# Expert weights of a two-layer mixer block loaded as pairs of tiles with 8 KB rows

## The chip, the cores and the metric

The kernel runs on one core of a Trainium2 chip. The metric is the device time of one execution in microseconds (us); less is better. TensorE, VectorE, ScalarE, GpSimd and SyncE are called PE, DVE, ACT, POOL and SP as the profile does; PEld is the weight load of a matmul.

## What is computed

Two layers of a hybrid mixer over 256 latent and 256 context tokens of width 1024. The change concerns the channel mixer of the second layer, which sends each of the 256 latent tokens to 2 of 8 experts:

```python
def _swiglu(h, w_gate, w_up, w_down):
    return (jax.nn.silu(h @ w_gate) * (h @ w_up)) @ w_down

def _moe(h, router, w_gate, w_up, w_down):
    t = h.reshape(-1, shape[-1])
    logits = (t @ router).astype(jnp.float32)
    top_val, top_idx = lax.top_k(logits, TOP_K)          # TOP_K = 2
    top_w = jax.nn.softmax(top_val, axis=-1)
    gate = jnp.sum(jax.nn.one_hot(top_idx, N_EXPERTS) * top_w[..., None], axis=1)
    out = jnp.zeros_like(t)
    for e in range(N_EXPERTS):                           # 8 experts, hidden width 3584
        out = out + gate[:, e:e + 1] * _swiglu(t, w_gate[e], w_up[e], w_down[e])
```

All weights are float32. One expert's three matrices are 44 MB, the eight together 352 MB.

## The kernel before

**The first 930 us** are layer 0 (attention, a gated recurrence, a gated spatial unit, a dense SwiGLU) and the mixers of layer 1. Their weights come through `Stream` (line 73): a raw 512 KB tile is loaded and split by ACT and DVE into a high and a low part, which PE multiplies in three passes. A scheduler sets the order of every engine there.

**Memory.** `Mem` (line 39) holds lists of free 4 KB, 2 KB and 1 KB slots (bytes per partition); a slot that is given back goes to the end of its list, and the next taker gets the one at the front. There are 34 slots of 4 KB from the start (line 1843). When the mixers of layer 1 are done, the pool of the small slots is closed and 16 more slots of 4 KB take its place (lines 1952 to 1954).

**The expert layer** (`moe_layer`, line 1964) loads every expert's weights whole and gathers the tokens of an expert (up to 96) by a matmul with a one-hot matrix (`moe_gather`, line 1537). An expert is four units: units 0 to 2 take 1024 hidden columns each, unit 3 the last 512. `gate_up` (line 1585) does the two input products of a unit in two halves, `turned` (line 1613) transposes the result on PE, and `moe_down` (line 1631) multiplies it with the rows of the output matrix one unit later. So a unit of 1024 columns consumes 16 weight tiles in `gate_up` and 8 in `moe_down`, unit 3 takes 8 and 4: 84 tiles of 512 KB for an expert, 672 in all. The matmuls take the weights as the moving operand, 512 (unit 3: 256) columns for 32 tokens, four column groups of PE side by side (`four`, line 1571).

An expert with at most 64 tokens can leave out a third of this work. `arms` (line 1578) writes both versions into the program and branches between them:

```python
        with self.tc.If(self.third[e] > 0) as c:
            yield 1
        with c.Else():
            yield 0
```

In this input experts 0, 2, 4, 6 and 7 take the long arm and experts 1, 3 and 5 the short one. `moe_add` (line 1668) scatters an expert's result back to the tokens with two blocks of four matmuls (`t<-yhl,ohT`, line 1682); it is a generator that `paced` (line 1972) moves on by one step for each step of `gate_up` and `moe_down`, and it begins only when `Mem` has two free slots (`mem.room`, line 1671). In the expert layer PE's order is the order of the program.

**The ring.** `Ring` (line 161) loads the expert weights in the order of a list that `moe_plan` (line 1770) makes. `need(n)` hands out the next n tiles and first gives back the slots of the tiles handed out before:

```python
    def load(self):
        while self.n_dma < len(self.plan) and self.free:
            slot = self.free.popleft()
            r = slot.tile([P, 1024], F32, name=f"wr{self.n_dma}")
            self.tiles[self.n_dma] = r, slot
            self.nc.sync.dma_start(r, self.plan[self.n_dma])
            self.n_dma += 1
```

It gets its slots in three steps: the three raw slots of `Stream` when its list is through (`heir`, line 136), 25 at line 1955 and 2 at line 1961, which leaves 14 slots to the rest of the expert layer. So the ring has 30 tiles. All its loads are issued by SP. Each DMA takes one of 8 semaphores in turn, and SP waits for the DMA that held it before, so at most 8 loads are under way.

Of the kernel before, what the change touches and what calls it, by code (L numbers as in the profile page):

```python
# [9 lines left out]
F32 = mybir.dt.float32  # L10
# [25 lines left out]
TTS = (2, 3, 0, 1)  # L36


class Mem:


    def __init__(self):
        self.free = {4: deque(), 2: deque(), 1: deque()}
        self.used = {}

    def add(self, pool, kb, n, mark=""):
        self.free[kb].extend(pool.ring(1024 * kb, name=f"m{mark}{kb}_{i}") for i in range(n))

    def get(self, kb, shape, name, dt=F32):
        slot = self.free[kb].popleft()  # L50
        n = int(np.prod(shape[1:]))
        t = slot.tile([P, (512 if dt == BF16 else 256) * kb], dt, name=name)[:, :n]
        if len(shape) > 2:
            d = "abcd"[:len(shape) - 1]
            t = t.rearrange(f"p ({' '.join(d)}) -> p {' '.join(d)}", **{x: int(m) for x, m in zip(d, shape[1:])})
        self.used[id(t)] = kb, slot, t
        return t
# [15 lines left out]
class Stream:  # L73
# [3 lines left out]
    def __init__(self, nc, plan, mem, raw, hl):  # L77
        self.nc, self.plan, self.mem = nc, plan, mem
        self.n_dma = self.n_split = self.n_out = self.n_done = self.part = 0
        self.raw, self.hl = {}, {}  # L80
        self.raw_free, self.hl_free = deque(), deque()
        self.heir = None
        self.excess = 0
        self.grow(raw, hl)

    def grow(self, raw, hl):

        free = self.mem.free[4]
        self.raw_free.extend(free.popleft() for _ in range(raw))
        self.hl_free.extend((free.popleft(), free.popleft()) for _ in range(hl))  # L90

    def close(self):

# [21 lines left out]
    def step(self):  # L115
        i, nc = self.n_split, self.nc
        w = self.plan[i][1]
        r, slot = self.raw[i]
        if self.part == 0:
            s = self.hl_free.popleft()  # L120
            self.hl[i] = [x.tile([P, 1024], F32R, name=f"{t}{i}") for x, t in zip(s, ("hi", "lo"))] + [s]
        h, l, _ = self.hl[i]
        s = slice(0, min(w, 512)) if self.part == 0 else slice(512, w)
        if s.stop > s.start:
            nc.scalar.activation(h[:, s], r[:, s], AF.Copy)  # L125
            nc.vector.tensor_tensor(l[:, s], r[:, s], h[:, s].bitcast(F32), op=ALU.subtract)  # L126
        self.part += 1
        if self.part == 2:
            self.part = 0
            self.n_split += 1  # L130
            del self.raw[i]
            if self.n_dma < len(self.plan):
                self.raw_free.append(slot)
                self.load()
            else:
                self.heir.free.append(slot)
                self.heir.load()

    def tick(self, n=1):
        for _ in range(n):  # L140
# [20 lines left out]
class Ring:  # L161
# [4 lines left out]
        self.n_dma = self.n_out = 0  # L166
        self.free, self.tiles, self.held = deque(), {}, []

    def grow(self, n):
        for _ in range(n):  # L170
            self.free.append(self.mem.free[4].popleft())
        self.load()

    def load(self):
        while self.n_dma < len(self.plan) and self.free:
            slot = self.free.popleft()
            r = slot.tile([P, 1024], F32, name=f"wr{self.n_dma}")
            self.tiles[self.n_dma] = r, slot
            self.nc.sync.dma_start(r, self.plan[self.n_dma])
            self.n_dma += 1  # L180

    def need(self, n):
# [6 lines left out]
        return [r for r, _ in got]  # L189

    def close(self):
        self.mem.free[4].extend(self.held)
        self.mem.free[4].extend(self.free)
        self.held, self.free = [], deque()


class Gen:
# [1387 lines left out]
    def gate_up(self, e, x, u, h):  # L1585


        nc = self.nc
        n = 512 if u < 3 else 256
        G, U, X = (self.psum("u") for _ in range(3))  # L1590
        for half in range(2):
            w = [t.rearrange("p (k n) -> p k n", k=2) for t in self.ring.need(8 if u < 3 else 4)]
            for arm in self.arms(e):
                for q in range(2):
                    v = w[4 * q:4 * q + 4] if u < 3 else [t[:, :, s:s + 256] for t in w[2 * q:2 * q + 2]
                                                          for s in (0, 256)]
# [34 lines left out]
    def moe_down(self, e, hT, u, yb, yx):  # L1631

        m = 4 if u < 3 else 2
        w = [(t[:, :512], t[:, 512:]) for t in self.ring.need(2 * m)]
        for arm in self.arms(e):
            if u == 0 and not arm:
                self.four(yx, 512, ((self.zero, w[0][0]),) * 4, True, True)
# [64 lines left out]
    def moe_rest_expert(self, one, off, n):  # L1702
# [14 lines left out]
        py = [self.psum("mm") for _ in range(2)]  # L1717
        for c in range(7):
            pgu = []
            for nm in ("moe_g", "moe_u"):  # L1720
                ps = self.psum("u")
                for kq in range(4):
                    r = load(A[nm][one, c, kq].rearrange("o p k n -> p (o k n)"))
# [15 lines left out]
            self.done(pt)  # L1739
            mem.put(h)  # L1740
            for a in range(4):
                r = load(A["moe_d"][one, 4 * c + a].rearrange("o p n -> p (o n)"))
# [27 lines left out]
    def moe_plan(self):  # L1770

        A = self.A
        f = lambda ap: ap.rearrange("p a b -> p (a b)")
        plan = []
        for i in range(len(self.UNITS) + 1):
            if i < len(self.UNITS):
                e, u = self.UNITS[i]
                cs = (2 * u, 2 * u + 1) if u < 3 else (6,)
                plan += [f(A[nm][e, c, kq]) for kq in range(4) for nm in ("moe_g", "moe_u") for c in cs]
            if i:  # L1780
                e, u = self.UNITS[i - 1]
                m = 4 if u < 3 else 2
                plan += [A["moe_d"][e, 8 * u + m * b + j] for j in range(m) for b in range(2)]
# [52 lines left out]
    def build(self):  # L1836
        nc, tc, A = self.nc, self.tc, self.A
        with ExitStack() as ctx:
# [4 lines left out]
            mem.add(big, 4, N4)  # L1843
# [10 lines left out]
            self.ring = self.ws.heir = Ring(nc, self.moe_plan(), mem)  # L1854
# [60 lines left out]
            self.run(self.norm_mod(0, 24, (0,)))  # L1915
            self.run(self.ffn(), self.ada_columns())
            self.run(self.norm_mod(1, 0, (0,)))
            self.begin(1)
            proj = self.proj(1)
            self.tokens()  # L1920
# [30 lines left out]
            mem.free[1].clear()  # L1951
            c1.close()
            more = ctx.enter_context(tc.tile_pool(name="more", bufs=1, side="right"))
            mem.add(more, 4, N4B, "x")
            self.ring.grow(len(mem.free[4]) - 5)
            self.run(self.prep_tile(1, w1, rows["ga"]))
            mem.put(*self.mxt, rows["ga"])
            self.ws.close()
            self.moe_prep(rows["sh"], rows["sc"])
            self.gf = rows["gf"]  # L1960
            self.ring.grow(len(mem.free[4]) - 14)
            self.moe_layer()

    def moe_layer(self):
# [48 lines left out]
NF = 2  # L2013
PVC = ((0,), (0, 2))
N4, N2, N1 = 34, 12, 24
N4B = 16
GROW0 = 4
FSHR = 2
PSPARE = dict(mm=0, u=2)
# [49 lines left out]
def _layout(inp):  # L2069
# [23 lines left out]
    for n, s in (("moe_g", "moe_w_gate"), ("moe_u", "moe_w_up")):  # L2093
        d[n] = c(g[s][0].reshape(NE, 4, 2, P, 7, 512).transpose(0, 4, 1, 3, 2, 5))
    d["moe_d"] = c(g["moe_w_down"][0].reshape(NE, 28, P, D))
# [22 lines left out]
```

## Time and profile before

| | |
|---|---|
| median of 3 runs | 1843.02 us (1839.42, 1843.02, 6153.94) |
| the profiled execution | 1835.17 us |
| its span, first to last instruction | 1833.4 us |
| PE busy in the span | 1753.2 us, 96% |
| mean granted TensorE clock | 0.988 |
| read from HBM | 481 MB |

The profiled execution is 7.8 us shorter than the median. Busy time of PE is the union of its matmuls, whose ends are modelled; the queue q1 of the DMA table carries what SP issues, q8 the blocks of instructions that the engines fetch. A row of the timeline merges instructions of one line; the bracket behind it tells how long the engine was idle before it and what ended that.

### The profile page before, as it was taken

How to read it: one execution, taken by the hardware profiler on the slowest of the kernel's cores; microseconds unless marked ns; L12 is line 12 of the kernel's file. 1: busy time of each engine (PE TensorE's matmuls, PEld its weight loads, DVE VectorE, ACT ScalarE, POOL GpSimd, SP SyncE). 2: the span in 40 equal slices, each digit the busy share in tenths (PEclk: the TensorE clock that was granted, in tenths of full speed). 3: DMA queues.
4: the chain of work that ended last, by engine and by line, in shares of the span. 5: the costliest groups of instructions: out<-in, count | busy, mean ns of one | idle time of the engine just before them, and what ended most of it. 6: DMA issues, size and time to landing. Idle time of an engine off the chain costs nothing. (4 is left out here: it accounts for less than half of the span.)

```text
span 1833.4 us, 34728 instructions
## 1 busy us (share of the span) xinstructions
PE 1753.2 (96%) x14056; PEld 1084.3 (59%) x14057; DVE 778.5 (42%) x1924; ACT 537.7 (29%) x1203; POOL 33.3 (2%) x56
## 2 busy tenths in 40 slices
PE   6999999999999999999989998999989999999996
PEld 3999778988788898998843333333333333333332
DVE  4656877899755377868720011110212011120112
ACT  4654655723223256765410010100101011010100
POOL 1000000100000001000000000000000000000000
PEclk9999999999999999999989999999999999999998
DMA  9224342366763245230589999999999999999990
GB/s 347 73 83 147 114 150 80 117 241 226 240 221 134 97 143 182 89 127 13 196 316 379 402 406 407 406 407 400 402 400 406 404 402 402 400 407 404 403 392 31
DMA packets 137006, 485.64 MB, mean 265 GB/s; under 512 B 15888, under 2 KB 17040, under 8 KB 136784
## 3 DMA queue, kind: packets, MB, share of 16 engines
q1 hardware_dynamic: 136080, 480.08, 69.1%
q8 instruction: 168, 2.75, 0.6%
q0 software_dynamic: 704, 2.36, 0.4%
q14 instruction: 54, 0.44, 0.1%
HBM read 481.33 MB, written 1.05 MB: 263 GB/s over the span
## 5 line engine op out<-in xcount | busy, mean ns | idle before, releaser
L1575 PE MATMUL u<-wr,xg 128*32 128x512 f32 (+1 forms) x5376 | 523.9, 545 | 19.7 <-issue 14.6
L1575 PEld LDWEIGHTS u<-wr,xg 128*32 128x32 f32 x5376 | 174.0, 111 | 342.2 <-issue 291.5
L1575 PE MATMUL mm<-wr,mT 128*32 128x512 f32 x2352 | 261.1, 593 | 3.8 <-ACT mh L264 1.5
L125 ACT ACTIVATE hi<-raw 128x512 fp32r<-128x512 f32 (+2 forms) x296 | 160.3, 580 | 247.1 <-PE u L246 84.8
L126 DVE TENSOR_TENSOR lo<-raw,hi 128x512 fp32r<-128x512 f32 (+2 forms) x296 | 178.9, 636 | 98.3 <-ACT hi L125 96.7
L1608 DVE TENSOR_TENSOR mh<-mh,u 128x512 f32<-128x512 f32 (+1 forms) x32 | 19.8, 619 | 410.9 <-PE u L1575 257.0
L1575 PEld LDWEIGHTS mm<-wr,mT 128*32 128x32 f32 x2352 | 77.8, 110 | 175.4 <-issue 149.7
L264 ACT ACTIVATE mh<-u 128x512 f32<-128x512 f32 (+1 forms) x64 | 34.6, 540 | 413.9 <-PE u L1575 413.3
L244 PE MATMUL u<-hx,hi 128*128 128x512 f32 (+1 forms) x384 | 142.9, 372 | 0.0
L245 PE MATMUL u<-hx,lo 128*128 128x512 f32 (+1 forms) x384 | 142.7, 372 | 0.0
L246 PE MATMUL u<-hx,hi 128*128 128x512 f32 (+1 forms) x384 | 142.7, 372 | 0.0
L264 ACT ACTIVATE mT<-t 128x512 f32<-128x512 f32 (+1 forms) x32 | 17.4, 544 | 256.3 <-PE t L1620 255.4
L245 PE MATMUL mm<-fx,lo 128*128 128x256 f32 (+1 forms) x264 | 85.7, 325 | 4.4 <-DVE lo L126 4.2
L244 PE MATMUL mm<-hi,hx 128*128 128x256 f32 x288 | 85.3, 297 | 4.2 <-ACT hx L264 3.9
L244 PE MATMUL mm<-fx,hi 128*128 128x256 f32 (+1 forms) x264 | 85.0, 322 | 0.6 <-ACT hi L125 0.6
L1626 DVE COPY mT<-t 128x256 f32<-128x256 f32 (+1 forms) x32 | 12.5, 392 | 170.6 <-PE t L1625 170.6
L246 PE MATMUL mm<-fx,hi 128*128 128x256 f32 (+1 forms) x264 | 84.6, 321 | 0.0
L245 PE MATMUL mm<-hi,hx 128*128 128x256 f32 x288 | 82.0, 286 | 0.6 <-DVE hx L521 0.3
L246 PE MATMUL mm<-lo,hx 128*128 128x256 f32 x288 | 81.7, 285 | 0.2 <-DVE lo L126 0.2
L246 PEld LDWEIGHTS u<-hx,hi 128*128 128x128 f32 x384 | 72.4, 188 | 12.6
L245 PEld LDWEIGHTS u<-hx,lo 128*128 128x128 f32 x384 | 72.4, 188 | 12.4
L244 PEld LDWEIGHTS u<-hx,hi 128*128 128x128 f32 x384 | 72.4, 188 | 12.4
(342 smaller groups left out, 2624.9 us busy)
## 6 DMA issues: line engine op xcount, KB each, us to landing
wr<-in_moe_g SPq DMA_DIRECT2D x224, 512.0 KB, 10.1
wr<-in_moe_u SPq DMA_DIRECT2D x224, 512.0 KB, 10.1
wr<-in_moe_d SPq DMA_DIRECT2D x224, 512.0 KB, 10.1
adat<-in_w_adaT SPq DMA_DIRECT2D x56, 512.0 KB, 5.0
raw<-in_ffn_gu SPq DMA_DIRECT2D x44, 512.0 KB, 3.5
adaw<-in_w_ada SPq DMA_DIRECT2D x40, 512.0 KB, 6.5
raw<-in_w_in SPq DMA_DIRECT2D x40, 512.0 KB, 3.5
raw<-in_ffn_d SPq DMA_DIRECT2D x24, 384.0 KB, 3.6
```

The lines of the kernel that those rows point to most:

```text
L125: nc.scalar.activation(h[:, s], r[:, s], AF.Copy)
L126: nc.vector.tensor_tensor(l[:, s], r[:, s], h[:, s].bitcast(F32), op=ALU.subtract)
L244: i = mm(ps, lh, rh, start=start, stop=False, skip_group_check=True)
L245: mm(ps, ll, rh, start=False, stop=False, skip_group_check=True)
L246: self.final = mm(ps, lh, rl, start=False, stop=stop, skip_group_check=True)
L264: i = self.nc.scalar.activation(out, in_, func, **kw)
L1575: self.nc.tensor.matmul(bank[c:c + 32, :n], lhsT, rhs, start=start, stop=stop, tile_position=(0, c), skip_group_check=True)
L1608: nc.vector.tensor_tensor(h[:, 0, :n], h[:, 0, :n], U[:, :n], op=ALU.mult)
L1626: nc.vector.tensor_copy(hT[:, :m, :, 64:], pt[:, :m * 64].rearrange("p (j a s) -> p j a s", j=m, a=2))
```

## The change

Gate and up weights are stored together (`moe_gu`), and the output rows two by two (`moe_d`), so that 128 partitions x 8 KB lie in one piece. The plan has 336 such pairs in place of 672 tiles, and the ring 18 pairs (36 tiles) in place of 30 tiles. The 16 late slots of 4 KB become 8 of 8 KB. Three more 8 KB buffers (`Twin`) stand among the 34 early slots; each is lent out as two halves of 4 KB until the ring takes it, and `Mem.slot` gives halves first to float32 takers up to layer 1 and last after it. The other 7 pairs are two single slots (`Pair`), each loaded by two DMAs of 4 KB rows. So 11 of 18 pairs come by one DMA with 8 KB rows. `Stream` gives its raw slots back to `Mem` and no longer to the ring. The ring takes all but 5 and then all but about 6 of the free slots, where it left 14.

```diff
+class Twin:
+    def __init__(self, buf):
+        self.buf = buf
+        self.halves = [Half(self, i) for i in range(2)]
+    def tile(self, shape, dt, name):
+        return self.buf[:, :]
+class Half:
+    def tile(self, shape, dt, name):
+        return self.twin.buf[:, 1024 * self.i:1024 * self.i + 1024]
...
+    def slot(self, kb, dt):
+        free = self.free[kb]
+        if kb == 4:
+            want = dt == F32 and not self.late
+            for x in free:
+                if isinstance(x, Half) == want:
+                    free.remove(x)
+                    return x
+            assert dt == F32
+        return free.popleft()
...
             else:
-                self.heir.free.append(slot)
-                self.heir.load()
+                self.mem.free[4].append(slot)
...
-    def grow(self, n):
-        for _ in range(n):
-            self.free.append(self.mem.free[4].popleft())
+    def grow(self, spare):
+        big, small = self.mem.free[8], self.mem.free[4]
+        while big:
+            self.free.append(big.popleft())
+        self.free.extend(self.mem.twins(spare))
+        while len(small) - 2 >= spare:
+            self.free.append(Pair(small.popleft(), small.popleft()))
         self.load()
     def load(self):
         while self.n_dma < len(self.plan) and self.free:
-            slot = self.free.popleft()
-            r = slot.tile([P, 1024], F32, name=f"wr{self.n_dma}")
-            self.tiles[self.n_dma] = r, slot
-            self.nc.sync.dma_start(r, self.plan[self.n_dma])
+            slot, ap, n = self.free.popleft(), self.plan[self.n_dma], self.n_dma
+            if isinstance(slot, Pair):
+                r = [x.tile([P, 1024], F32, name=f"wr{n}") for x in slot.slots]
+                for z in range(2):
+                    self.nc.sync.dma_start(r[z], ap[:, 1024 * z:1024 * z + 1024])
+            else:
+                t = slot.tile([P, 2048], F32, name=f"wr{n}")
+                self.nc.sync.dma_start(t, ap)
+                r = [t[:, 1024 * z:1024 * z + 1024] for z in range(2)]
+            self.tiles[n] = r, slot
             self.n_dma += 1
...
-            w = [t.rearrange("p (k n) -> p k n", k=2) for t in self.ring.need(8 if u < 3 else 4)]
+            w = [[t.rearrange("p (k n) -> p k n", k=2) for t in r] for r in self.ring.need(4 if u < 3 else 2)]
...
-        w = [(t[:, :512], t[:, 512:]) for t in self.ring.need(2 * m)]
+        w = [(t[:, :512], t[:, 512:]) for r in self.ring.need(m) for t in r]
...
-            mem.add(more, 4, N4B, "x")
-            self.ring.grow(len(mem.free[4]) - 5)
+            mem.add(more, 8, N8B, "x")
+            self.ring.grow(5)
             self.run(self.prep_tile(1, w1, rows["ga"]))
             mem.put(*self.mxt, rows["ga"])
             self.ws.close()
+            self.ring.grow(6)
             self.moe_prep(rows["sh"], rows["sc"])
             self.gf = rows["gf"]
-            self.ring.grow(len(mem.free[4]) - 14)
...
-N4B = 16
+N8, N8B = 3, 8
```

Which matmul reads which tile, and the number of PE, DVE, ACT and POOL instructions, stay the same. Two places where the order moves:

PE, in the short-arm expert 1: its unit 3, before. `u` are the banks of the input products, `t<-yhl,ohT` is a block of the scatter of expert 0; the rows begin at the end of the first half of the unit.

```order
L1575 MATMUL u_110<-wr_11724,xg 32x256 x4
L1580 UNCONDITIONAL_BRANCH
L1682 MATMUL t_106<-yhl,ohT 128x512 x2
L1682 MATMUL t_107<-yhl,ohT 128x512 x2
L1580 COMPARE_AND_BRANCH
L1575 MATMUL u_108<-wr_11726,xg 32x256 x4
```

The same block now: it stands between the halves of unit 0 of expert 2, whose matmuls have 512 columns.

```order
L1639 MATMUL u_105<-wr_11615,xg 32x512 x2
L1644 UNCONDITIONAL_BRANCH
L1748 MATMUL t_103<-yhl,ohT 128x512 x2
L1748 MATMUL t_104<-yhl,ohT 128x512 x2
L1644 COMPARE_AND_BRANCH
L1639 MATMUL u_108<-wr_11618,xg 32x512 x2
```

The block has moved back by one unit and a half, from an expert with the short arm into the next one with the long arm; the second block of the same scatter moves in the same way, and so do those of experts 2 and 4.

SP, where the ring starts, before: the last raw tiles of layer 1 (`in_w_out`) and the first tiles of the ring, in slots that came free one by one.

```order
L112 DMA raw_9442<-in_w_out 128x1024
L179 DMA wr_9693<-in_moe_u 128x1024
L179 DMA wr_9699<-in_moe_u 128x1024
L179 DMA wr_9719<-in_moe_g 128x1024
L179 DMA wr_9713<-in_moe_g 128x1024
L112 DMA raw_9457<-in_w_out 128x1024
L179 DMA wr_9701<-in_moe_u 128x1024
L112 DMA raw_9501<-in_w_out 128x1024
```

Now, the same place; a row with 128x2048 is a load with 8 KB rows.

```order
L166 DMA twin_64<-in_w_out 128x1024 x2
L241 DMA twin_66<-in_moe_gu 128x2048
L238 DMA wr_9514<-in_moe_gu 128x1024
L238 DMA wr_9594<-in_moe_gu 128x1024
L166 DMA twin_65<-in_w_out 128x1024
L238 DMA wr_9515<-in_moe_gu 128x1024
L166 DMA twin_64<-in_w_out 128x1024
L241 DMA twin_65<-in_moe_gu 128x2048
L238 DMA wr_9523<-in_moe_gu 128x1024
L241 DMA wr_9495<-in_moe_gu 128x2048
```

Six DMAs of the ring, with the bytes of eight tiles, now stand ahead of the first of the eight late 8 KB buffers (`wr_9495`), which hold the pairs that PE needs first.

## Rows read from the trace of the kernel before

**Rows 1.** The page, part 1: busy time of the engines over the span.

```profile
PE 1753.2 (96%) x14056; PEld 1084.3 (59%) x14057; DVE 778.5 (42%) x1924; ACT 537.7 (29%) x1203; POOL 33.3 (2%) x56
```

**Rows 2.** Windows: layer stretch, three expert pairs; PE, PEld, DVE, ACT, POOL, clock, DMA share, GB/s.

```profile
200.00:900.00 700.00, 689.59 (x4368) 602.75 (x4367) 522.42 (x1319) 340.03 (x790) 20.75 (x30) 1.00 0.43 143
1046.50:1261.90 215.40, 205.48 (x1956) 73.46 (x1956) 30.70 (x50) 20.60 (x40) 0.00 (x0) 0.99 1.02 405
1261.90:1479.30 217.40, 206.23 (x1956) 73.28 (x1956) 30.70 (x50) 20.61 (x40) 0.00 (x0) 0.99 1.02 404
1479.30:1694.30 215.00, 207.35 (x1956) 73.95 (x1956) 29.31 (x45) 20.30 (x40) 0.00 (x0) 0.98 1.02 403
```

**Rows 3.** Waits of SP's DMA queue: waited for, us in total, times, longest.

```profile
SPq L179 <- DMA wr<-in_moe_g: 171.2, 186, 2.6
SPq L179 <- DMA wr<-in_moe_d: 167.0, 190, 2.4
SPq L179 <- DMA wr<-in_moe_u: 157.3, 187, 2.4
SPq L179 <- PE u L1575: 68.9, 53, 7.7
```

**Rows 4.** Tile wr: time from issue to landing.

```profile
DMA to landing us min/median/max: 3.4/10.1/11.8
```

**Rows 5.** DMA issues from 790 us to 1105.5 us.

```profile
wr<-in_moe_g SPq DMA_DIRECT2D x56, 512.0 KB, 9.1
wr<-in_moe_u SPq DMA_DIRECT2D x56, 512.0 KB, 8.3
wr<-in_moe_d SPq DMA_DIRECT2D x44, 512.0 KB, 8.9
```

**Rows 6.** DMA issues from 790 us to 1577 us.

```profile
wr<-in_moe_g SPq DMA_DIRECT2D x176, 512.0 KB, 10.1
wr<-in_moe_u SPq DMA_DIRECT2D x176, 512.0 KB, 10.1
wr<-in_moe_d SPq DMA_DIRECT2D x164, 512.0 KB, 10.1
```

**Rows 7.** Timeline of PE, end of expert 1: start us, us, what, idle before.

```profile
1124.49 1.93 PE L1575 MATMUL u<-wr,xg 128*32 128x256 f32 x32 [1.26 <-issue]
1126.35 1.19 PE L1682 MATMUL t<-yhl,ohT 96*128 96x512 f32 x4
1131.31 5.35 PE L1575 MATMUL u<-wr,xg 128*32 128x256 f32 x64 [3.77 <-DMA wr<-in_moe_g]
1136.59 1.19 PE L1682 MATMUL t<-yhl,ohT 96*128 96x512 f32 x4
1137.71 7.07 PE L1575 MATMUL mm<-wr,mT 128*32 128x512 f32 x64
```

**Rows 8.** Source line L1580 on PE's sequencer: ns min/median/max.

```profile
L1580 PEldq COMPARE_BRANCH  x156: 65/184/6152, 936.2 to 1812.5; - x156
```

**Rows 9.** Timeline of PE, expert 6 (first row) and what follows.

```profile
1578.77 20.81 PE L1575 MATMUL u<-wr,xg 128*32 128x512 f32 x192
...
1625.75 1.20 PE L1682 MATMUL t<-yhl,ohT 96*128 96x512 f32 x4
...
1638.89 0.66 PE L1620 MATMUL t<-ident,mh 128*128 128x128 f32 x4 [0.38 <-DVE xt L1684]
```

**Rows 10.** DMA queues from 1062 to 1146 us.

```profile
DMA packets 9327, 34.14 MB, mean 406 GB/s; under 512 B 1032, under 2 KB 1032, under 8 KB 9312
...
q1 hardware_dynamic: 9312, 33.92, 101.5%
q8 instruction: 12, 0.20, 1.0%
```

**Rows 11.** DMA queues from 1792 to 1815 us, after the last load.

```profile
q8 instruction: 4, 0.07, 1.2%
```

**Rows 12.** DMA queues from 473.4 to 473.9 us: one packet of 8 KB.

```profile
q14 instruction: 1, 0.01, 3.9%
```

More of the change, by code (lines that the diff above doesn't have):

```diff
@@ L36, with __init__, add_twins, twins @@
 TTS = (2, 3, 0, 1)
+class Twin:
[5 more added lines that the diff above has]
+class Half:
+    def __init__(self, twin, i):
+        self.twin, self.i = twin, i
+    def tile(self, shape, dt, name):
+        assert dt == F32
+        return self.twin.buf[:, 1024 * self.i:1024 * self.i + 1024]
+class Pair:
+    def __init__(self, *slots):
+        self.slots = slots
 class Mem:
     def __init__(self):
-        self.free = {4: deque(), 2: deque(), 1: deque()}
+        self.free = {8: deque(), 4: deque(), 2: deque(), 1: deque()}
         self.used = {}
+        self.late = False
     def add(self, pool, kb, n, mark=""):
         self.free[kb].extend(pool.ring(1024 * kb, name=f"m{mark}{kb}_{i}") for i in range(n))
+    def add_twins(self, pool, n):
+        h = [x for i in range(n) for x in Twin(pool.tile([P, 2048], F32, name=f"twin{i}")).halves]
+        self.free[4].extend(h)
+    def twins(self, spare):
+        free = self.free[4]
+        got = []
+        for t in {id(x.twin): x.twin for x in free if isinstance(x, Half)}.values():
+            if len(free) - 2 >= spare and all(h in free for h in t.halves):
+                for h in t.halves:
+                    free.remove(h)
+                got.append(t)
+        return got
+    def slot(self, kb, dt):
[6 more added lines that the diff above has]
+                    return x
+            assert dt == F32
+        return free.popleft()
     def get(self, kb, shape, name, dt=F32):
-        slot = self.free[kb].popleft()
+        slot = self.slot(kb, dt)
         n = int(np.prod(shape[1:]))
@@ L81, in __init__ @@
         self.raw_free, self.hl_free = deque(), deque()
-        self.heir = None
         self.excess = 0
@@ L86, in grow @@
     def grow(self, raw, hl):
-        free = self.mem.free[4]
-        self.raw_free.extend(free.popleft() for _ in range(raw))
-        self.hl_free.extend((free.popleft(), free.popleft()) for _ in range(hl))
+        m = self.mem
+        self.raw_free.extend(m.slot(4, F32) for _ in range(raw))
+        self.hl_free.extend((m.slot(4, F32R), m.slot(4, F32R)) for _ in range(hl))
     def close(self):
@@ L191, in close @@
     def close(self):
-        self.mem.free[4].extend(self.held)
-        self.mem.free[4].extend(self.free)
+        for slot in self.held + list(self.free):
+            self.mem.free[4].extend(slot.halves if isinstance(slot, Twin) else slot.slots if isinstance(slot, Pair) else ())
         self.held, self.free = [], deque()
@@ L1591, in gate_up @@
         for half in range(2):
-            w = [t.rearrange("p (k n) -> p k n", k=2) for t in self.ring.need(8 if u < 3 else 4)]
+            w = [[t.rearrange("p (k n) -> p k n", k=2) for t in r] for r in self.ring.need(4 if u < 3 else 2)]
             for arm in self.arms(e):
                 for q in range(2):
-                    v = w[4 * q:4 * q + 4] if u < 3 else [t[:, :, s:s + 256] for t in w[2 * q:2 * q + 2]
-                                                          for s in (0, 256)]
+                    if u < 3:
+                        v = [r[z] for z in range(2) for r in w[2 * q:2 * q + 2]]
+                    else:
+                        v = [w[q][z][:, :, s:s + 256] for z in range(2) for s in (0, 256)]
                     for k in range(2):
@@ L1719, in moe_rest_expert @@
             pgu = []
-            for nm in ("moe_g", "moe_u"):
+            for nm in range(2):
                 ps = self.psum("u")
                 for kq in range(4):
-                    r = load(A[nm][one, c, kq].rearrange("o p k n -> p (o k n)"))
+                    r = load(A["moe_gu"][one, c, kq][:, :, nm].rearrange("o p k n -> p (o k n)"))
                     for k in range(2):
@@ L1741, in moe_rest_expert @@
             for a in range(4):
-                r = load(A["moe_d"][one, 4 * c + a].rearrange("o p n -> p (o n)"))
+                i = self.down_rows().index(4 * c + a)
+                r = load(A["moe_d"][one, i // 2][:, :, i % 2].rearrange("o p n -> p (o n)"))
                 for dh in range(2):
@@ L1772, in moe_plan @@
         A = self.A
-        f = lambda ap: ap.rearrange("p a b -> p (a b)")
         plan = []
@@ L1778, in moe_plan, with down_rows @@
                 cs = (2 * u, 2 * u + 1) if u < 3 else (6,)
-                plan += [f(A[nm][e, c, kq]) for kq in range(4) for nm in ("moe_g", "moe_u") for c in cs]
+                plan += [A["moe_gu"][e, c, kq].rearrange("p z k n -> p (z k n)") for kq in range(4) for c in cs]
             if i:
                 e, u = self.UNITS[i - 1]
-                m = 4 if u < 3 else 2
-                plan += [A["moe_d"][e, 8 * u + m * b + j] for j in range(m) for b in range(2)]
-        return plan
+                plan += [A["moe_d"][e, 4 * u + j].rearrange("p b n -> p (b n)") for j in range(4 if u < 3 else 2)]
+        return plan
+    @staticmethod
+    def down_rows():
+        return [8 * u + m * b + j for u, m in ((0, 4), (1, 4), (2, 4), (3, 2)) for j in range(m) for b in range(2)]
     def load_X(self):
@@ L1842, in build @@
             mem = self.mem = Mem()
-            mem.add(big, 4, N4)
+            mem.add_twins(big, N8)
+            mem.add(big, 4, N4 - 2 * N8)
             c1 = ExitStack()
@@ L1853, in build @@
             self.ws = Stream(nc, self.plan(), mem, RAW1, SP1)
-            self.ring = self.ws.heir = Ring(nc, self.moe_plan(), mem)
+            self.ring = Ring(nc, self.moe_plan(), mem)
             self.sil = little.tile([P, KD, 32], F32, name="sil")
@@ L1917, in build @@
             self.run(self.norm_mod(1, 0, (0,)))
+            mem.late = True
             self.begin(1)
@@ L2092, in _layout @@
     d["ffn_d"] = c(g["ffn_w_down"][0].reshape(2, 11, P, 8, P).transpose(0, 3, 2, 1, 4))
-    for n, s in (("moe_g", "moe_w_gate"), ("moe_u", "moe_w_up")):
-        d[n] = c(g[s][0].reshape(NE, 4, 2, P, 7, 512).transpose(0, 4, 1, 3, 2, 5))
-    d["moe_d"] = c(g["moe_w_down"][0].reshape(NE, 28, P, D))
+    d["moe_gu"] = c(np.stack([g[s][0].reshape(NE, 4, 2, P, 7, 512).transpose(0, 4, 1, 3, 2, 5)
+                              for s in ("moe_w_gate", "moe_w_up")], 4))
+    d["moe_d"] = c(g["moe_w_down"][0].reshape(NE, 28, P, D)[:, Gen.down_rows()].reshape(NE, 14, 2, P, D)
+                   .transpose(0, 1, 3, 2, 4))
     d["router"] = c(g["moe_router"][0].reshape(KD, P, NE).transpose(1, 0, 2))
```

## The prediction

> **What bounds the kernel now.** I read the busy times first: PE works in 96% of the span [rows 1], so the question is what holds it in the stretch that the change touches. The windows answer for three pairs of experts, each a long-arm and a short-arm one [rows 2]: PE is busy for 205.5 of 215.4 us, 206.2 of 217.4 and 207.4 of 215.0, and in the same stretches the DMA engines are busy all the time (share 1.02, 403 to 405 GB/s). Both look full, and they nearly are: a pair needs 168 tiles of 512 KB, 88.1 MB, at 405 GB/s 217.5 us. SP too seems to say that loads bind, since it waits 171 + 167 + 157 = 495 us for earlier loads and only 69 us for the input products of PE to free a slot [rows 3]. But this tells of the queue, not of PE. Whether PE waits for a weight is seen by laying landings against use.
>
> I do this at two places. A tile lands at most 11.8 us after its issue [rows 4]. By 1105.5 us 56 + 56 + 44 = 156 tiles are issued [rows 5], landed by 1117.3. These are all that the second half of unit 3 of expert 1 needs (two experts, 168, less the 12 of the last two `moe_down`). PE starts that half at 1131.31, after an idle time of 3.77 us [rows 7]: its weights had been there for 14 us. The name of a load in that row's bracket is that of an event that happened to fall there. What did hold PE is the branch: the row of line 1580 has branches of up to 6152 ns on PE's sequencer with a median of 184 [rows 8]. The instruction queue moves 0.20 MB in 12 packets in 84 us of the short arm [rows 10], so 16 KB a packet, some 7 us apart. PE jumps over the long arm and must fetch what stands behind it. The Trainium skill ("Runtime: NRT & Kernel Launch", Instruction fetch mechanics) says that instructions come in blocks of 16 KiB and that a taken branch to a block not at hand stalls until it is fetched; the trace agrees in the 16 KB and in the stall.
>
> The tightest place is the start of expert 6. By 1577 us 176 + 176 + 164 = 516 tiles are issued [rows 6], landed by 1588.8. The second half of its unit 0 needs them, about 20.81 / 2 us after 1578.77 [rows 9], at 1589.2. The spare time has shrunk to about half a microsecond, but the 192 matmuls of the unit run without a gap. So PE and its branches set the pace, and the loads keep up, only just. All idle time of PE in the three pairs is 9.9 + 11.2 + 7.7 = 28.7 us [rows 2]; no faster load can give back more there.
>
> **The change, part by part.**
>
> *8 KB rows.* Bytes stay the same. In 84 us the load queue has 9312 packets, 1032 of them the small completion writes, so 8280 rows of 4 KB; 101.5% of 16 x 84 us are 1364 us, 165 ns a row, 329 for two [rows 10]. An 8 KB load is not in the trace. The nearest row is an 8 KB packet of another queue: 3.9% of 16 x 0.5 us, 312 ns [rows 12]. So 8 KB cost between 312 and 329 ns; I take 312, the one row of that size. Of the 336 pairs the new order loads 209 (62%) whole. A pair of experts then needs 217.5 x (1 - 312/329) x 0.62 = 7.0 us less of DMA time. PE does not wait for it, so this is worth nothing: the loads are only earlier. If the loads did bind, it would be worth 3 x 7.0 = 21 us.
>
> *A ring of 36 tiles.* It deepens a lead that already suffices: nothing.
>
> *The start of the ring.* The pairs that PE needs first now lie in the late 8 KB buffers, behind six DMAs with the bytes of eight tiles. In the trace the corresponding late slots are filled well before the first half ends; with 1.3 us a tile (88.1 MB in 217.5 us for 168) these eight take 10 us and the first unit's 16 tiles 21. The first half needs only eight of them. I take nothing; at worst the 10 us in front come whole.
>
> *Fewer free slots.* With 6 or 7 slots left in place of 14, `moe_add` of experts 0, 2 and 4 finds its two slots later. Its two blocks of four matmuls leave the unit 3 of the short arm, where the first lies beside a branch fetch: 1126.35 + 1.19 is 1127.54, and PE idles on to 1131.31 [rows 7], so taking it out saves nothing. The second is followed by `moe_down` 1.12 us after its start (1136.59 to 1137.71) with a branch in the same place; taking it out saves 0 to 1.1 us, I take 0.6. They now stand in the next long-arm expert, where PE has no gaps: 1.20 us each, as the blocks of the odd experts there do, and after a second block the transpose waits 0.38 us for DVE [rows 9]. For three experts: 3 x (2 x 1.20 + 0.38 - 0.6) = +6.5 us. The ends are 0 (they land beside a fetch again) and 3 x (2.4 + 0.4) = 8.4.
>
> *The first 930 us.* `Mem.slot` hands out other slots, so some instructions change places, and a few loads wait for a half that was used more recently. PE has 700 - 689.6 = 10.4 us of gaps from 200 to 900 us [rows 2]. I take 0, with 10 either way. `Stream` splits from three raw slots as before.
>
> *Instruction fetch beside longer rows.* The fetch shares the DMA engines with the loads. A packet takes 1.0% of 16 x 84 us / 12 = 1.12 us beside full loads [rows 10] and 1.2% of 16 x 23 us / 4 = 1.10 us with no load at all [rows 11]. So rows of 4 KB cost the packet itself hardly anything; I take nothing for 8 KB. The lower end is 0; the upper is that the idle time of PE doubles, +29 us.
>
> The sum is +6.5 us. On the profiled execution, 1835.2 us, that is 1841.7. The median of the runs shown is 7.8 us above the profiled one, so I put the forecast at 1843 + 6 = 1849.
>
> **Rivals.**
>
> *A, the loads bind after all.* For it: DMA share 1.02 and 495 us of SP's waits. Against it: the 14 us of spare time in the very idle time that bears a load's name. Then 21 us come back, less 6.5: 1843 - 14.5, about 1828. Even all 28.7 us of idle time, with the moved blocks free, give 1814, which is under 2%. The Trainium skill ("DMA: Bandwidth & Descriptors", Rules for kernel authors) asks for 1 MiB and more in a DMA for the highest rate. By that rule this rival's loads would be faster, but no run here shows a 1 MiB load yet.
>
> *B, the branches get longer: slower.* A branch fetch needs several turns at a DMA engine (descriptor, data, completion), and each may stand behind a row that is twice as long. The short arm needs 12 fetches in 84 us, and its stalls follow one another. With 0.8 us more for each of the 12 fetches of three short-arm experts: 3 x 12 x 0.8 = 29 us, 1843 + 29 + 6 = 1878. From 0.9 us a fetch on it is slower by over 2%. Against it stand 1.12 and 1.10 us; for it, that the packet's own time does not show the wait before it.
>
> *C, the first part stalls* on halves that are taken again too early, or the first unit on its late buffers: +10 us each, 1843 + 6 + 20 = 1869.
>
> *D, 8 KB rows cost as much as two of 4 KB.* Then only the moved blocks are left, and the time is that of the forecast.
>
> **How the numbers follow.** A measurement of this kernel can tell about 2%, 37 us, from no change: under 1806 or over 1880. Forecast with D 0.66, A 0.15, B 0.12, C 0.07. Faster by over 2% needs more than all of PE's idle time in the pairs: 0.03. Slower by over 2% takes half of B and a little of C: 0.08. The rest, 0.89, is within 2%. The range goes from a little below A, 1824, to B, 1878.
>
> **What would show it.** Right: PE's idle time before the second half of unit 3 in experts 1, 3 and 5 is still 3 to 4 us; SP's waits move from earlier loads to PE, since the ring is now full; the share of the DMA engines falls below 1 in the pairs, which still take 215 to 220 us; blocks of four `t<-yhl,ohT` stand in unit 0 of experts 2, 4 and 6. Wrong: pairs of 210 us or less with the share still 1 would mean A; branches of line 1580 well over 6.2 us, with longer short arms, would mean B; an expert layer that starts later than 936 us would mean C.

## The result, and the profile after

| | before | after |
|---|---|---|
| median, us (6 runs each) | 1840.64 | 1853.32 |
| range without one disturbed run of before | 1836.38 to 1843.02 | 1851.05 to 1859.62 |
| span of the profiled execution | 1833.4 | 1849.3 |

The ratio is 1.0077, interval 1.0055 to 1.0099: within 2%, but longer by about 13 us. The forecast was 1849 us, 1824 to 1878, for a change of +6.5 us. Which terms make up the measured change is another matter.

The busy time of the changed kernel over the span, beside [rows 1]:

```profile
PE 1757.8 (95%) x14056; PEld 1089.3 (59%) x14057; DVE 777.6 (42%) x1924; ACT 537.0 (29%) x1203; POOL 33.0 (2%) x56
```

The windows of the same stretches, beside [rows 2] (PE, PEld, DVE, ACT, POOL, clock, DMA share, GB/s), and expert 5 alone, before and after:

```profile
200.00:900.00 700.00, 688.24 (x4375) 602.78 (x4375) 523.41 (x1320) 341.17 (x793) 20.43 (x30) 1.00 0.43 144
1044.40:1260.40 216.00, 206.69 (x1960) 75.17 (x1960) 30.94 (x51) 20.64 (x41) 0.00 (x0) 0.98 1.01 410
1260.40:1479.80 219.40, 207.15 (x1960) 74.71 (x1962) 30.64 (x50) 20.39 (x40) 0.00 (x0) 0.98 1.01 405
1479.80:1711.10 231.30, 212.12 (x1960) 76.44 (x1961) 29.30 (x45) 20.19 (x40) 0.00 (x0) 0.97 0.97 382
...
1479.30:1578.80 99.50, 93.23 (x836) 34.41 (x837) 14.93 (x23) 11.11 (x24) 0.00 (x0) 0.97 1.02 402
1479.80:1592.50 112.70, 95.97 (x824) 35.84 (x824) 12.20 (x19) 10.77 (x24) 0.00 (x0) 0.94 0.99 395
```

Most of the loss has one address. The expert layer starts 1.8 us earlier than before (934.5 against 936.3), the three pairs take 0.6, 2.0 and 16.3 us more, and the last expert takes the same 120.9. Of the 16.3 us, expert 5 has 13: its short arm took 99.5 us before. The rest fits the moved blocks: experts 2, 4 and 6, in which they now stand, take 1.9, 2.3 and 3.1 us more, experts 1 and 3, which they left, 1.2 and 0.3 us less. The short arm idles for 7 us in expert 1, 10 in expert 3 and 17 in expert 5.

SP's waits, beside [rows 3]:

```profile
SPq L241 <- PE u L1639: 280.2, 75, 9.3
SPq L241 <- PE mm L1639: 90.7, 44, 5.4
SPq L238 <- PE u L1639: 86.0, 45, 6.2
...
SPq L238 <- DMA wr<-in_moe_gu: 46.6, 36, 2.8
```

SP now waits mostly for PE to free a slot: the ring is full, so the weights are further ahead than before. PE still idles at the place of [rows 7], the second half of unit 3 of expert 1:

```profile
1121.86 1.93 PE L1639 MATMUL u<-wr,xg 128*32 128x256 f32 x31 [0.86 <-issue]
1128.05 6.40 PE L1639 MATMUL u<-wr,xg 128*32 128x256 f32 x59 [4.26 <-issue]
```

In expert 5 it idles there too (4.53 us), and at four more places, each for about 2 us or more, every one of them "issue", that is, with nothing that it is seen to wait for:

```profile
1505.28 9.57 PE L1639 MATMUL u<-wr,xg 128*32 128x512 f32 x64
1514.78 1.57 PE L1898 MATMUL t<-oh,mhf 128*128 128x192 f32 x8
1518.53 5.34 PE L1639 MATMUL u<-wr,xg 128*32 128x512 f32 x32 [2.17 <-issue]
...
1544.31 4.45 PE L1639 MATMUL u<-wr,xg 128*32 128x512 f32 x34 [2.73 <-issue]
...
1551.55 7.07 PE L1639 MATMUL u<-wr,xg 128*32 128x512 f32 x64 [2.43 <-issue]
...
1576.74 1.34 PE L1639 MATMUL u<-twin,xg 128*32 128x256 f32 x16 [4.53 <-issue]
...
1583.20 8.77 PE L1639 MATMUL mm<-wr,mT 128*32 128x512 f32 x64 [1.98 <-issue]
```

The granted clock of this expert is 0.94, and 64 matmuls that take 7.07 us elsewhere take 9.57 and 8.77. In four stretches of 3.4 us, from 1505.7, 1519.4, 1577.4 and 1584.2 us on, it is 0.50, the lower of its two levels (1.2 of 2.4 GHz); each begins within 2 us of the end of an idle time of 1.9 to 4.5 us. The branches of the line beside [rows 8] are hardly longer than before at the most, but expert 5 now has three over 4 us (6.2, 6.1 and 4.4), where it had one (5.5):

```profile
L1644 PEldq COMPARE_BRANCH  x156: 65/186/6201, 934.1 to 1829.2; - x156
```

The rows of 8 KB are what was forecast. In 84 us of the first pair:

```profile
DMA packets 6468, 34.67 MB, mean 413 GB/s; under 512 B 713, under 2 KB 713, under 8 KB 3785
...
q1 hardware_dynamic: 6453, 34.44, 100.5%
q8 instruction: 13, 0.21, 1.0%
```

3785 - 713 = 3072 rows of 4 KB at the 165 ns of before take 507 us of the 100.5% of 16 x 84 us, so the 6453 - 3785 = 2668 rows of 8 KB take 844 us, an estimate of 316 ns each; 312 was taken. The moved blocks stand where forecast too, here in unit 0 of expert 4:

```profile
1371.60 1.20 PE L1748 MATMUL t<-yhl,ohT 96*128 96x512 f32 x4
```

### The profile page after: what moved, and what is told of

Its sections match the earlier page's. It is cut to its first block, busy times and chain, and to the rows that moved or that the text cites. A ratio compares the mean times of both kernels' runs of the same rounds, so it can differ in the third digit from the quotient of the medians.

```text
span 1849.3 us, 34250 instructions
## 1 busy us (share of the span) xinstructions
PE 1757.8 (95%) x14056; PEld 1089.3 (59%) x14057; DVE 777.6 (42%) x1924; ACT 537.0 (29%) x1203; POOL 33.0 (2%) x56
## 5 line engine op out<-in xcount | busy, mean ns | idle before, releaser
L1639 PE MATMUL u<-wr,xg 128*32 128x512 f32 (+1 forms) x4312 | 452.7, 549 | 21.9 <-issue 20.7
L1639 PEld LDWEIGHTS u<-wr,xg 128*32 128x32 f32 x4312 | 151.1, 112 | 266.8 <-issue 237.6
L1639 PE MATMUL mm<-wr,mT 128*32 128x512 f32 x2096 | 232.8, 596 | 4.8 <-ACT mh L328 2.8
L179 ACT ACTIVATE hi<-twin 128x512 fp32r<-128x512 f32 (+2 forms) x296 | 160.6, 581 | 254.4 <-PE u L310 90.7
L180 DVE TENSOR_TENSOR lo<-twin,hi 128x512 fp32r<-128x512 f32 (+2 forms) x296 | 178.5, 634 | 99.7 <-ACT hi L179 98.5
L1639 PEld LDWEIGHTS mm<-wr,mT 128*32 128x32 f32 x2096 | 70.1, 110 | 155.9 <-issue 140.2
L1639 PE MATMUL u<-twin,xg 128*32 128x512 f32 (+1 forms) x1064 | 131.2, 546 | 8.7 <-issue 8.7
L1639 PEld LDWEIGHTS u<-twin,xg 128*32 128x32 f32 x1064 | 40.2, 110 | 86.5 <-issue 79.0
L1750 DVE SCALAR_TENSOR_TENSOR xt<-t,gate,xt 128x512 f32<-128x512 f32 x32 | 22.6, 747 | 157.7 <-PE t L1748 157.6
L309 PEld LDWEIGHTS u<-hx,lo 128*128 128x128 f32 x384 | 72.3, 188 | 12.6
```

The costliest lines, as they stand in the source:

```text
L309: mm(ps, ll, rh, start=False, stop=False, skip_group_check=True)
L1639: self.nc.tensor.matmul(bank[c:c + 32, :n], lhsT, rhs, start=start, stop=stop, tile_position=(0, c), skip_group_check=True)
L1750: nc.vector.scalar_tensor_tensor(self.xt[tt][:, s], ps, gate[:, tt], self.xt[tt][:, s], op0=ALU.mult, op1=ALU.add)
```

## The experiments

All ratios are to the kernel before, run beside them on the same chip, where its medians were 1837.5 to 1838.2 us.

**One part of the change at a time.** *4 KB rows in the changed kernel*: the order of PE, DVE and ACT is the same, instruction for instruction.

```
-                self.nc.sync.dma_start(t, ap)
+                for z in range(2):
+                    self.nc.sync.dma_start(t[:, 1024 * z:1024 * z + 1024], ap[:, 1024 * z:1024 * z + 1024])
```

> The changed kernel with each of the 209 whole pairs loaded by two DMAs of 4 KB rows in place of one of 8 KB rows; slots, order and the work of PE stay. Before: 1841 us, after: 1853 us. Theory 1 (PE and its branches set the pace, row size is worth nothing): 1853 us, within 4 us. Rival (the 8 KB rows hold up the instruction fetch, and that is the 13 us that expert 5 lost): about 1841 us, with no branch over 5.5 us in expert 5. Rival A (loads bind, and the 8 KB rows help): up to 21 us longer, 1860 to 1874 us.

1837.5 us, 0.9989 (0.9976 to 1.0002), so in this kernel the pairs loaded by two DMAs are 16 us faster. The third pair, and in it expert 5:

```profile
1477.50:1694.70 217.20, 208.23 (x1960) 74.83 (x1961) 29.30 (x45) 20.18 (x40) 0.00 (x0) 0.98 1.02 403
...
1477.50:1577.40 99.90, 92.15 (x828) 34.25 (x831) 12.20 (x19) 10.84 (x24) 0.00 (x0) 0.95 1.02 403
```

Theory 1 missed, and the rival came in: no branch in expert 5 takes more than 2.5 us. But "the longer rows hold up the fetch" is not yet shown: where a pair comes as two DMAs, PE also executes 52 separate semaphore waits in the expert layer in place of 32, and its code lies a little elsewhere.

*14 free slots in the changed kernel*: `self.ring.grow(6)` becomes `self.ring.grow(12)`.

> The changed kernel with three pairs fewer in the ring (15 pairs, 30 tiles, as before), so that 14 slots stay free and the moe_add blocks of experts 0, 2 and 4 stand in unit 3 of the short arm again; the 8 KB rows stay. Theory 1 (the moved blocks cost 6.5 us, the rest is where the branches fall): 1841 to 1847 us. Rival (the longer rows hold up the fetch): 1847 us or more, with branches over 6 us in expert 5 still. Rival (the deeper ring is worth something): longer than 1853 us. Rival A: if loads bound, the 8 KB rows without the moved blocks would give 1820 to 1830 us.

1832.4 us, 0.9964 (0.9947 to 0.9981): 21 us below the changed kernel, 6 below the one before, and between theory 1 and rival A. With the same long rows the whole change is no loss here. That suggests that their price hangs on the code around them; this kernel was not run with 4 KB rows.

*The moved blocks and the deep ring in the kernel before*: `len(mem.free[4]) - 14` becomes `- 8`.

> The kernel before with six tiles more in the ring (36 tiles of 4 KB rows) and 8 free slots, as after: the moe_add blocks of experts 0, 2 and 4 move into unit 0 of the next expert, and nothing else of the change is in. Theory 1: 1841 + 6.5 = 1847 us. If the moved blocks also shift the code so that expert 5 meets its fetches worse, as it does after: 1853 us, with two branches of about 6 us in expert 5. Rival (the longer rows are the cause of the loss): 1841 us, within 3 us. Rival A (a deeper ring helps): under 1838 us.

1842.1 us, 1.0022 (1.0008 to 1.0036): +4 us, where 6.5 were forecast. This lies between theory 1 and the rival (within 3 us) and does not part them. The branches of experts 1 to 6 are 3.3 us at most, and expert 5 takes 98.2 us, so moving the blocks does not bring its stalls by itself.

**Do weights or code hold PE?** *Half of the loads left out*:

```
-        while self.n_dma < len(self.plan) and self.free:
+        while self.n_dma < len(self.plan) and (self.free or self.n_dma % 2):
+            if self.n_dma % 2:
+                self.tiles[self.n_dma] = self.tiles[self.n_dma - 1][0], None
+                self.n_dma += 1
+                continue
```

> The changed kernel with every second pair of weight tiles not loaded: its matmuls read the pair before it, so half of the experts' weights are left out of the result and half of the bytes out of the DMA, while PE has the same matmuls. Theory 1 (weights are always there; fetches take as long beside loads as without): within 5 us of 1853 us, PE idle in experts 1, 3 and 5 still 7 to 17 us each. Rival A (PE waits for weights): the idle time goes, 1853 - 30 = 1823 us or less, with the branches of line 1644 as long as before. Rival B (the fetches stand behind loads): also shorter, by 10 to 30 us, but with the long branches gone.

1879.8 us, 1.0215: longer, and this says nothing of loads. With other loads the scheduler put the output chain of an expert ahead of the product `mh` on DVE, and PE's transposes waited for it:

```profile
L1690 PE MATMUL t<-ident,mh 128*128 128x128 f32 x85 | 16.2, 310 | 28.4 <-DVE mh L1678 28.4
```

*The same with the order held*, by adding DVE and ACT to `tc.manual_schedule`:

> As the run with half of the weight loads left out (the matmuls of every second pair read the pair before it), but with DVE and ACT in the order of the program text in the expert layer, so that the product that PE's transposes wait for does not stand behind the output chain. Theory 1 (no wait for weights; the stalls are of the fetch): 1830 to 1850 us, and PE idles in experts 1, 3 and 5 for 4 us or more each, released by nothing. Rival A (loads bind): all idle time of PE in them goes, 1815 us or less.

1823.3 us, 0.9909 (0.9887 to 0.9932). Groups of PE in the three pairs:

```profile
L1643 PE MATMUL u<-wr,xg 128*32 128x512 f32 (+1 forms) x3248 | 317.6, 541 | 9.2 <-issue 9.2
L1643 PE MATMUL mm<-wr,mT 128*32 128x512 f32 x1392 | 156.5, 603 | 6.6 <-issue 6.6
L1643 PE MATMUL u<-twin,xg 128*32 128x512 f32 (+1 forms) x592 | 59.3, 536 | 2.0 <-issue 2.0
L1643 PE MATMUL mm<-twin,mT 128*32 128x512 f32 x288 | 33.4, 619 | 3.1 <-issue 3.1
```

Neither theory: 7 us below the first, 8 above rival A. With half of the bytes, 21 us of idle time without a cause in the profile remain, and none ends with a load. So what remains is no wait for weights. What has gone has no single cause here: the order of DVE and ACT changed too, and the fetch is faster beside fewer loads. Of the records of the instruction queue in the three pairs, the tenth percentile of the time from one 16 KB packet to the next is 4.0 us here. It is 5.8 before, 5.75 after and 5.8 with 4 KB rows: the *length* of a row does not matter to this fastest pace.

**Where the blocks end.** 32 or 64 matmuls on zeros ahead of the experts shift PE's code:

```
+        ps = self.psum("t")
+        for _ in range(32):
+            nc.tensor.matmul(ps[:32, :32], self.zero, self.zero, start=True, stop=True)
+        self.done(ps)
```

> The changed kernel with 32 matmuls of 32x32 on zeros more, ahead of the first gather of the experts. They shift the code of PE behind them by 64 instructions, a part of one 16 KB block; the order of all engines, the loads and their 8 KB rows stay. The matmuls themselves cost 1 to 3 us, ahead of the expert layer. Theory P (where the blocks' ends fall against the branches sets the stalls of expert 5): expert 5, 112.7 us after, comes to 98 to 104 us here or in the run with 64 of them, and that run takes 1838 to 1846 us. Theory R (the 8 KB rows hold up the fetch, wherever the blocks end): expert 5 stays at 110 us or more in both, and both take 1853 to 1858 us.

> The changed kernel with 64 such matmuls, 128 instructions of PE, and nothing else. Theory P: the time and the stalls of expert 5 differ from those with 32 and with none by more than 4 us, in either direction. Theory R: 1854 to 1860 us, expert 5 at 110 us or more.

The expectations count two instructions for each of these matmuls; the chip executes four, two matmuls and two weight loads. The counts of the two runs show it, beside x14056 and x14057 after:

```profile
PE 1758.2 (96%) x14120; PEld 1090.8 (59%) x14121; DVE 776.9 (42%) x1924; ACT 537.6 (29%) x1203; POOL 33.1 (2%) x56
```

```profile
PE 1764.3 (95%) x14184; PEld 1094.6 (59%) x14185; DVE 778.4 (42%) x1924; ACT 537.4 (29%) x1203; POOL 33.1 (2%) x56
```

A packet of 16 KB holds 256 instructions (worked out below). So 32 of them, 128 instructions, shift the code by half a packet, and 64 by a whole one, after which the packets end at the same instructions as without them.

With 32: 1846.0 us, 1.0048 (1.0032 to 1.0063). With 64: 1852.0 us, 1.0076 (1.0061 to 1.0091). Expert 5 with 32, then with 64:

```profile
1484.70:1582.40 97.70, 90.96 (x825) 34.12 (x824) 12.50 (x20) 11.00 (x25) 0.00 (x0) 0.98 1.02 412
```

```profile
1487.80:1597.50 109.70, 94.25 (x829) 35.30 (x827) 12.50 (x20) 11.05 (x25) 0.00 (x0) 0.94 1.01 403
```

With 32, work was added and the ratio fell by 0.3%, 5 us, though the intervals overlap: with 8 KB rows and the same order, a shift by half a packet takes expert 5 from 112.7 to 97.7 us in the profiled executions, where theory R had 110 or more. With 64, twice the work was added, and expert 5 is back at 109.7 us and the ratio at that of the changed kernel. For 64, theory P had said a time unlike both; it missed by its count of instructions, and a shift by a whole packet that changes nothing speaks for placement. The other experts of the run with 32 are up to 1.7 us slower, and it is still 8 us above the kernel before, at the far edge of what theory P said.

The records of the instruction queue show what is lost. In the short arms, experts 1, 3 and 5, the time from one packet to the next is over 10 us three times after (12.6 in expert 3, 13.2 and 12.3 in expert 5), three times with 64 (12.7, then 12.8 and 10.7) and never with 32 (9.5 at most). It is once with 14 free slots (13.0 in expert 5), and never in the three kernels with 4 KB rows, 8.8 us at most: before, after with 4 KB rows, and before with 8 free slots. So placement is a cause with 8 KB rows; whether the rows are one as well is not shown.

**The jumps themselves.** *One branch for both halves of gate_up*, with DVE and ACT in the order of the text:

```
-        for half in range(2):
-            w = [... for r in self.ring.need(4 if u < 3 else 2)]
-            for arm in self.arms(e):
-                for q in range(2):
+        w = [... for r in self.ring.need(8 if u < 3 else 4)]
+        for arm in self.arms(e):
+            for q in range(4):
```

> The changed kernel with one branch for each gate_up in place of one for each half (8 branches an expert in place of 12), so that PE jumps over 384 instructions at a time; both halves' pairs are taken together, and DVE and ACT keep the order of the program text in the expert layer. If the stalls come from the fetch of code that is jumped over: the idle time of PE in experts 1, 3 and 5, 33 us after, falls to under 15 us, and the time to about 1835 us. If the loads then bind, since 8 pairs must be there at once: idle time that ends with a DMA, and 1845 us or more. If the number of branches does not matter: 1850 to 1856 us.

1916.1 us, 1.0426 (1.0412 to 1.044): the idea was wrong, and by its sign. In expert 3:

```profile
1314.70 6.18 PE L1639 MATMUL u<-twin,xg 128*32 128x512 f32 x34 [5.56 <-issue]
...
1348.50 12.78 PE L1639 MATMUL u<-wr,xg 128*32 128x512 f32 x96 [5.76 <-issue]
```

After a jump over 384 instructions PE stood here for about the time from one packet to the next. The Trainium skill ("Runtime: NRT & Kernel Launch", Instruction fetch mechanics) says that a taken branch out of the two 16 KiB blocks at hand forces a fetch; the 5.56 and 5.76 us agree. It also calls the crossing of a block mostly hidden; the changed kernel with short jumps, below, agrees: in its three pairs no idle time of PE ends with "issue".

*Short jumps*: what both arms do stands in front of the branch, the third block alone inside it. In `moe_down` likewise, with `yx` zeroed in both arms.

```
-            for arm in self.arms(e):
-                ...
-                        if arm:
-                            self.four(X, n, ((b2, ga), (b2, gb), (b2, ua), (b2, ub)), *z)
+            todo = []
+                ...
+                    todo.append((((b2, ga), (b2, gb), (b2, ua), (b2, ub)), z))
+            with self.tc.If(self.third[e] > 0):
+                for parts, z in todo:
+                    self.four(X, n, parts, *z)
```

In the changed kernel:

> The changed kernel with the matmuls that both arms share put in front of the branch, and only those of the third block inside it: PE jumps over at most 32 matmuls and 32 weight loads, and the code of the short arm stands once less. If the stalls are those of the fetch behind a jump: the idle time released by nothing in experts 1, 3 and 5, 27 us after, falls to under 6 us, no branch over 2 us, and 1853 - 27 = 1826 us; PE then takes about 207 us a pair, less than the 210 us that loads of 8 KB rows need, so some waits for DMA may come: up to 1836 us. Rival (jumps cost the same whatever their length): 1850 us or more.

In the kernel before:

> The kernel before with the same edit: 4 KB rows, 30 tiles, blocks in place. PE would take about 207 us a pair, and loads of 4 KB rows need 217.5 us. If loads become the bound, a pair takes 213 us or more and PE's idle time ends with a DMA: 1830 to 1841 us. If they do not: 1841 - 20 = 1821 us or less.

In the changed kernel with 14 free slots:

> The same edit on the changed kernel with 15 pairs (14 free slots, 8 KB rows, blocks in place). If the longer rows pay once PE no longer waits for code: faster than the same edit on the kernel before by 5 us or more, 1815 to 1825 us. If they are worth nothing even then: the two agree within 4 us.

And in the changed kernel with 4 KB rows:

> The kernel of the run before with the short jumps on the changed kernel (1814 us), with each whole pair loaded by two DMAs of 4 KB rows; slots, ring and order stay. If the loads bind once PE no longer waits for code, the longer rows are what makes 1814 of 1828 us, and they are gone here: 1822 us or more, with waits for DMA. If the deeper ring and the placement made it: 1814 us, within 4 us.

| with short jumps | us | ratio |
|---|---|---|
| before: 4 KB rows, 30 tiles | 1827.6 | 0.9947 (0.9933 to 0.9960) |
| after, 4 KB rows, 36 tiles | 1818.8 | 0.9897 (0.9881 to 0.9914) |
| after, 30 tiles | 1817.0 | 0.9897 (0.9879 to 0.9914) |
| after | 1813.6 | 0.9868 (0.9850 to 0.9887) |

The three pairs of the last, of the changed kernel with 4 KB rows, and of the kernel before, all with short jumps:

```profile
1043.90:1250.90 207.00, 203.67 (x1965) 74.60 (x1964) 30.81 (x50) 20.71 (x41) 0.00 (x0) 1.00 1.02 414
1250.90:1458.00 207.10, 203.81 (x1970) 75.18 (x1969) 30.83 (x50) 20.76 (x41) 0.00 (x0) 1.00 1.02 412
1458.00:1672.00 214.00, 206.70 (x1969) 72.99 (x1970) 29.77 (x46) 20.71 (x41) 0.00 (x0) 1.00 1.01 411
```

```profile
1042.90:1250.00 207.10, 203.61 (x1969) 73.56 (x1969) 30.84 (x50) 20.78 (x41) 0.00 (x0) 1.00 1.03 407
1250.00:1459.40 209.40, 205.07 (x1965) 74.80 (x1964) 30.83 (x50) 20.63 (x41) 0.00 (x0) 1.00 1.02 406
1459.40:1678.10 218.70, 208.90 (x1969) 71.15 (x1968) 29.78 (x46) 20.77 (x41) 0.00 (x0) 1.00 1.02 405
```

```profile
1047.40:1253.90 206.50, 203.24 (x1966) 72.84 (x1964) 30.82 (x50) 20.68 (x41) 0.00 (x0) 1.00 1.03 407
1253.90:1469.10 215.20, 208.66 (x1970) 71.54 (x1969) 30.83 (x50) 20.79 (x41) 0.00 (x0) 1.00 1.03 406
1469.10:1686.70 217.60, 211.03 (x1966) 75.10 (x1966) 29.77 (x46) 20.71 (x41) 0.00 (x0) 1.00 1.03 406
```

The changed kernel gains 40 us, 13 more than the 27 of its idle time alone: PE is also busy for 12 us less in the three pairs, at a clock that stays up (1.00 in all of them). "Issue" is gone from PE's idle time, no branch of the three pairs is over 0.5 us, and the last pairs run into the loads: 88.1 MB at 411 GB/s are 214.4 us, at 405 to 406 GB/s 217 us, and they take 214.0, 218.7 and 217.6. The waits of PE in the kernel before with short jumps, second and third pair, name the loads (us in total, times, longest):

```profile
PE u L1575 <- DMA wr<-in_moe_u: 3.6, 11, 0.6
PE mm L1575 <- DMA wr<-in_moe_d: 2.6, 11, 0.4
```

The first pairs don't, since the ring starts full; so the kernel before came out between its two expectations. Now the change pays: 14 us, of which the rows are 5 (1818.8 to 1813.6, between the two expectations, 8 or more and at most 4) and the rest the deeper ring and the other parts of the change. With 30 tiles it is 10.6 us below the kernel before with the same edit, as was expected if the longer rows pay. The changed kernel with short jumps is 1.3% below the kernel before as it was.

## Why the prediction was right, and where it was not

- *The time*: 1849 us came near 1853 in part by luck. The sum was +6.5 us and the change +13, so half of it is not in the sum; and the forecast started from a median of 1843 us, which six runs put at 1840.6.
- *PE and its branches set the pace, the loads keep up, only just*: right. With half of the loads the idle time of PE that was left did not end with a load, and with short jumps the stalls went; as soon as they had, a pair of 4 KB rows took 217.6 us, where 217.5 were worked out.
- *8 KB rows are a little cheaper and worth nothing*: the size was right (316 ns for 312), the worth was wrong. Taking them out of this kernel saved 16 us, with 14 free slots the whole change saved 6, and with short jumps they save 5.
- *Fewer free slots, +6.5 us*: +4.0, interval 1.5 to 6.6, inside its ends 0 and 8.4. In the changed kernel experts 1 to 4 and 6 together give +5.8. With the stalls gone the blocks only change sides: expert 2 takes 117.1 us with them and 114.6 without, expert 1 89.9 and 92.1.
- *The first 930 us, the start of the ring*: nothing, as forecast (934.5 against 936.3); rival C falls.
- *Instruction fetch beside longer rows: nothing, upper end +29*. This is the step that failed: taken as 0, it stands against the 13 us of expert 5. It looked at the packet's own time, and rival B at the wait of each packet. The first stayed (a median of 1.07 us after, 1.08 before), and so did the fastest pace. What the step lacked is that in the short arm the fetch is itself at its limit: the 7 us that the prediction read from packet to packet are as long as half a unit. The three pairs of before, from 1045 to 1690 us, have 89 packets of the instruction queue:

```profile
q8 instruction: 89, 1.46, 0.9%
```

A pair has some 7,600 instructions in both arms, so 7600 x 3 / 89 = 256 a packet, and jumped-over code is fetched with the rest. A half of `gate_up` is 160 matmuls in both arms and as many weight loads, 320 instructions: 320 / 256 x 5.8 = 7.2 us of fetch, by estimate. The short arm runs it in 7.07 us, in unit 3 in half of that. The missing 3.7 us fit the 3.77 of [rows 7] and the 4.26 after. In units 0 to 2 the two are level, so where a block ends can decide whether a jump finds its target fetched; the two gaps of 13.2 and 12.3 us in expert 5 look like two that did not. With short jumps there are 57 packets in the same window:

```profile
q8 instruction: 57, 0.93, 0.6%
```

- *What would show it*: the idle time in unit 3 (4.26, 4.25 and 4.53 us, where 3 to 4 were said) and SP's waits came nearly as said. The share of the DMA engines did not fall below 1 in the first two pairs, and the third took 231 us, not 215 to 220. Rival A's rule of larger DMAs (the Trainium skill, "DMA: Bandwidth & Descriptors", Rules for kernel authors) can now be seen: 411 to 414 GB/s with 62% of the pairs whole, 405 to 407 in halves, both with short jumps. It agrees, for a gain of under 2%.
- *Open*: how much of the 13 us in expert 5 is the place of the code and how much the length of the rows beside it. The three kernels with 4 KB rows take 98.2 to 99.9 us there, each with its code at another place; the four with 8 KB rows 97.7 (32 matmuls), 101.9 (14 free slots), 109.7 and 112.7. So the rival that only the longer rows let the stalls grow, at some places of the code, is not ruled out. No run changed the rows with the code at the same place.

## What to carry to other kernels

Where a branch chooses between two whole versions of a loop, count all the code that lies between two jumps against the rate at which it is fetched, and not only what runs: put what both versions share in front of the branch and skip only the difference. While an engine is held by its instruction fetch, an edit ahead that only shifts its code can move the time: here 32 idle matmuls took 15 us from one expert, and 64 gave 12 of them back. A change to the loads is hard to judge there; take the stalls out first, and judge it then.

## What the runs showed of the hardware

- Instruction packets of 16 KB follow one another on PE seldom faster than 5.8 us (the tenth percentile) beside full loads, of 4 or of 8 KB rows, and 4.0 us beside half of them.
- Branches with a jump of at most 64 instructions behind them took up to 0.5 us in the changed kernel and 1.0 in the kernel before, those with 256 or 384 up to 6.8 us.
- The spread of the runs went with the stalls: 1851 to 1860 us with them, 1812 to 1814 without.
